# Decay matrices of a chunked delta rule: masked by an added matmul, or clipped on ScalarE and selected on GpSimd

## The chip, the core and the metric

The kernel runs on one core of one Trainium2 chip. The metric is device microseconds of one launch. The times of before come from three runs; the profile comes from one more execution, taken by the hardware profiler.

## The reference, cut to what matters

The program is two transformer-like blocks on a sequence of 512 tokens with width 1024. The first block mixes by a gated delta rule in 8 heads, forward and backward, with a context of 256 tokens whose final states start the 512 tokens; beside it runs a pooling mixer. The second block is two layers of feed-forward, attention, convolution and a gate. The change touches only the delta rule's decay matrix:

```python
g = jnp.cumsum(g.reshape(bsz, nh, n, CHUNK), axis=-1)
incl = jnp.tril(jnp.ones((CHUNK, CHUNK), bool))
decay = jnp.exp(jnp.where(incl, g[..., :, None] - g[..., None, :], -jnp.inf))
a_mat = jnp.where(strict, jnp.einsum('bhncd,bhnsd->bhncs', kb, k) * decay, 0.0)
...
qk = jnp.einsum('bhncd,bhnsd->bhncs', q, k) * decay
```

Within a chunk, the decay from one token to another is the exponential of a difference of running sums, and zero where the second token isn't before or at the first. The kernel takes chunks of 128 tokens in the place of 64, which gives the same outputs: 2 chunks of context and 4 of the sequence, 6 in all per head and direction.

## The kernel before, in words

Everything lies with channels on the 128 partitions and tokens on the free axis. Every large product is made of three matmuls on operands split into a rounded part and a rest (`mm3`, lines 153 to 158: the rounded weights with both parts of the input, then the rest of the weights). `Stream` (lines 83 to 129) brings the weights in 512 KB pieces (`wraw`, three buffers) and splits each half on ScalarE (`whi`, line 108) and VectorE (`wlo`, line 109), with raised priority.

The first block (`block1`, line 799) prepares constants (lines 842 to 902), norms and modulation, and the gates of all heads at once (lines 1031 to 1079): `G` holds the running sums of g, with tokens on partitions, one column for each of 6 chunks and 16 pairs of direction and head; `GT` holds the same with tokens on the free axis, as two rounded parts.

Then it goes through 8 heads. The steps of a head are `k_in` (project k, convolve it, transpose it, norms), `pre` (decay matrices and the triangular inverse), `v_in`, `q_in` and `weights` (the products of q and k times the decay); in between stand `zproj`, `merge`, `chains` and `finish` of the head before, in the order of `STEPS = 'kzmpvcqwf'` (line 703). `merge` builds the inverse of a 128x128 triangular matrix from its 16x16 blocks in three levels, on TensorE (lines 1263, 1268, 1274) with ScalarE and VectorE between; `chains` runs the 6 chunks forward and backward.

`pre` (line 1179) makes, for each direction d, the tile `e` (E, 128 x 6 x 128). A matmul (line 1192) with a selecting column as weights spreads one row of `GT` over all partitions in PSUM (`Ep`, the pool `mis` of two buffers, 2 chunks and then 4); a second matmul (line 1194) adds the mask, 0 or -2^100, with the identity as weights and the mask repeated along the chunks as the moving operand. Line 1197 then takes Exp of each chunk on ScalarE, with the negated running sum of the row as bias. After both directions, B is E[1] times beta (ScalarE, line 1200), plus E[0] times beta (VectorE, line 1202), times the products of k with itself (`KK`, lines 1206 and 1207). B's 16x16 diagonal blocks go to DRAM and back in another layout (lines 1208 to 1217), VectorE inverts them in 15 steps (lines 1219 to 1221), and DMAs bring the results through DRAM into the diagonals of `Pm` and `Qm` (lines 1226 to 1236), which GpSimd has filled with zeros (line 1232). `merge` of this head works on them, one head later. `E` is also read by `weights` (line 1244).

The tiles E, B, P and Q have two buffers each per tag, and the convolved k (`kT`) of even and odd heads lies in two buffers in turn, so the copy of k for head N+2 (in `conv5`, line 1091) waits for the chains of head N.

The order on each engine's queue is fixed when the program is built: instructions whose operands are expected to be ready are taken by their place in the source, so that matmuls of projections stand between those of merge and chains. All DMAs of these steps are issued from SyncE's queue, in which the loads of the weights also stand.

Of the kernel before, what the change touches and what calls it, by code (L numbers as in the profile page):

```python
# [8 lines left out]
F32R = mybir.dt.float32r  # L9
AF = mybir.ActivationFunctionType  # L10
ALU = mybir.AluOpType
PSUM = bass.MemoryType.PSUM

P = 128
# [18 lines left out]
NEG = -float(2 ** 100)  # L33
# [765 lines left out]
def block1(tc, kk, W, h, xp, hp, xt, ctxt, par1, po, rcnt, prep2):  # L799


    nc = tc.nc
    with ExitStack() as ctx:
        cp = ctx.enter_context(tc.tile_pool(name="b1c", bufs=1))
# [13 lines left out]
        def tmp(name="t", shape=(P, S), dt=F32):  # L818
            return tp.tile(list(shape), dt, tag="t", name=name, bufs=5)
# [22 lines left out]
        def triangle(dst, op, fill, pattern, base=0, cm=1, init=0.0):  # L842
            nc.gpsimd.memset(dst, init)
            nc.gpsimd.affine_select(out=dst, in_=dst, compare_op=op, fill=fill, base=base,
                                    pattern=pattern, channel_multiplier=cm)

        cons = {}
        for d in range(2):
            t = tmp("tri", (P, P))

            triangle(t, ALU.is_ge, 0.0, [[1, P] if d == 0 else [-1, P]], cm=-1 if d == 0 else 1, init=1.0)
            cons["tri", d] = t
            m = tmp("m", (P, P))
            triangle(m, ALU.is_ge, NEG, [[1, P] if d == 0 else [-1, P]], cm=-1 if d == 0 else 1)
            mr = cp.tile([P, P], F32R, name=f"maskr{d}")
            nc.vector.tensor_copy(mr, m)
            cons["maskr", d] = mr
        for b in (16, 32, 64):

            g = 64 // b  # L860
# [3 lines left out]
            for t in range(2):  # L864
                lo = b if t == 0 else 0
                nc.gpsimd.affine_select(out=mv[:, :, t], in_=mv[:, :, t], compare_op=ALU.is_ge, fill=0.0, base=-lo,
                                        pattern=[[-2 * b, g], [0, b]], channel_multiplier=1)
                nc.gpsimd.affine_select(out=mv[:, :, t], in_=mv[:, :, t], compare_op=ALU.is_ge, fill=0.0, base=lo + b - 1,
                                        pattern=[[2 * b, g], [0, b]], channel_multiplier=-1)
# [7 lines left out]
        for base in (0, -64):  # L877
            nc.gpsimd.affine_select(out=zt, in_=zt, compare_op=ALU.not_equal, fill=1.0, base=base,
                                    pattern=[[-1, 16]], channel_multiplier=1)
        nc.vector.tensor_copy(zs, zt)  # L880
        DD = []
        for i in range(1):
# [5 lines left out]
                                    pattern=[[1, 16], [-1, 16]], channel_multiplier=0)  # L888
# [4 lines left out]
        cm = sp.tile([P, 2 * KD + 30], F32, name="cm")  # L893
# [146 lines left out]
        def gcol(name):  # L1040
            return sp.tile([P, 6, 16], F32, name=name)
# [13 lines left out]
        for d in range(2):  # L1055
            nc.tensor.matmul(pg[:, d * 48:d * 48 + 48], lhsT=cons["tri", d], rhs=g_[:, :, 8 * d:8 * d + 8], start=True, stop=True)
        nc.tensor.matmul(pg[:, 96:192], lhsT=onesm, rhs=g_, start=True, stop=True)
        G, negG, eG, negeG, etail, egl = (gcol(n) for n in ("G", "negG", "eG", "negeG", "etail", "egl"))
        for d in range(2):
            nc.vector.tensor_copy(G[:, :, 8 * d:8 * d + 8], pg[:, d * 48:d * 48 + 48].rearrange("p (c r) -> p c r", r=8))  # L1060
        gl = pg[:, 96:192].rearrange("p (c r) -> p c r", r=16)
        nc.vector.tensor_scalar(negG, G, -1.0, None, op0=ALU.mult)
        nc.scalar.activation(eG, G, AF.Exp)
        nc.vector.tensor_scalar(negeG, eG, -1.0, None, op0=ALU.mult)
        nc.vector.tensor_tensor(etail, gl, G, op=ALU.subtract)
# [113 lines left out]
        def pre(st):  # L1179


            hd = st.hd
            kc = [st.kT[:, tok(c)] for c in range(6)]
            st.E = E = []
            for d in range(2):
                r = 8 * d + hd
                e = cp.tile([P, 6, P], F32, tag="E", name="E", bufs=2)
                E.append(e)
                for a, b in ((0, 2), (2, 6)):
                    n = (b - a) * P  # L1190
                    ps = pmis("Ep")
                    nc.tensor.matmul(ps[:, :n], lhsT=zs[:, r:r + 1].to_broadcast([80, P]), rhs=GT[:, a * P:b * P],
                                     start=True, stop=False)
                    nc.tensor.matmul(ps[:, :n].rearrange("p (c r) -> p c r", r=P), lhsT=kk.identr,
                                     rhs=cons["maskr", d].unsqueeze(1).to_broadcast([P, b - a, P]), start=False, stop=True)
                    for c in range(a, b):
                        nc.scalar.activation(e[:, c], ps[:, (c - a) * P:(c - a) * P + P], AF.Exp, bias=negG[:, c, r:r + 1])
            st.B = cp.tile([P, 6, P], F32, tag="B", name="B", bufs=2)
            for c in range(6):
                scaled("B", st.B[:, c], E[1][:, c], st.ga[:, 0, c, 1:2])  # L1200
            for c in range(6):
                nc.vector.scalar_tensor_tensor(st.B[:, c], E[0][:, c], st.ga[:, 0, c, 0:1], st.B[:, c], op0=ALU.mult, op1=ALU.add)
            for a, b in ((0, 2), (2, 6)):
                ps = pmis("KK")
                for c in range(a, b):
                    nc.tensor.matmul(ps[:, (c - a) * P:(c - a) * P + P], lhsT=kc[c], rhs=kc[c], start=True, stop=True)
                nc.vector.tensor_tensor(st.B[:, a:b], st.B[:, a:b], ps[:, :(b - a) * P].rearrange("p (c r) -> p c r", r=P), op=ALU.mult)
            db = dp.tile([6, 8, 16, 16], F32, tag="db", name="db")
            for b in range(8):
                s = slice(16 * b, 16 * b + 16)  # L1210
                nc.sync.dma_start(db[:, b].rearrange("m r c -> r m c"), st.B[s, :, s])

            lt, X = DD[0]
            lr = tmp("lr")[0:48, :256].rearrange("p (r c) -> p r c", c=16)
            nc.sync.dma_start(lr, db.rearrange("m b r c -> (m b) r c"))
            nc.sync.dma_start(lt[64:112], db.rearrange("m b r c -> (m b) r c"))
            nc.vector.tensor_copy(lt[0:48], lr.rearrange("p r c -> p c r"))
            T = tmp("T")[0:112, :256].rearrange("p (r c) -> p r c", c=16)
            for i in range(1, 16):
                nc.vector.tensor_tensor(T[:, :i, :i], lt[:, i, :i].unsqueeze(2).to_broadcast([112, i, i]), X[:, :i, :i], op=ALU.mult)  # L1220
                nc.vector.tensor_reduce(X[:, i, :i], T[:, :i, :i].rearrange("p j c -> p c j"), axis=AX, op=ALU.add, negate=True)

            XT = tmp("XT")[0:112, :256].rearrange("p (r c) -> p r c", c=16)
            nc.vector.tensor_copy(XT, X.rearrange("p r c -> p c r"))

            st.P = cp.tile([P, 6, 2, P], F32, tag="P", name="Pm", bufs=2)
            st.Q = cp.tile([P, 6, 2, P], F32, tag="Q", name="Qm", bufs=2)
            for dst, f, w in ((st.P, (1, XT), (0, X)), (st.Q, (0, X), (1, XT))):
                dq = dp.tile([6, 2, 8, 16, 16], F32, tag="dq", name="dq")
                for p0, (t, y) in ((0, f), (64, w)):  # L1230
                    nc.sync.dma_start(dq[:, t].rearrange("m b r c -> m b (r c)"), y[p0:p0 + 48].rearrange("p r c -> p (r c)"))
                nc.gpsimd.memset(dst, 0.0)
                fl = dst.rearrange("p c t r -> p (c t) r")
                for b in range(8):
                    s = slice(16 * b, 16 * b + 16)
                    nc.sync.dma_start(fl[s, :, s], dq[:, :, b].rearrange("m t r c -> r (m t) c"))
# [342 lines left out]
```

## Time and profile before

| | |
|---|---|
| median of 3 runs | 2981.84 us (2981.61 to 2983.72) |
| the profiled execution, its time | 2982.64 us |
| its span, first to last instruction | 2980.9 us |
| TensorE busy | 2935.6 us, 98% |
| VectorE busy | 1914.2 us, 64% |
| ScalarE busy | 1302.4 us, 44% |
| GpSimd busy | 48.1 us, 2% |
| DMA | 268.77 MB, 90 GB/s in the mean |
| granted clock of TensorE, mean | 0.995 of 2.4 GHz |

The span goes from the first to the last instruction of the program; the time of the execution lies a little above it. PE is TensorE's matmuls, PEld its loads of weights (beside them), DVE VectorE, ACT ScalarE, POOL GpSimd, SP SyncE; a q behind the name is the engine's sequencer. The ends of matmuls are modelled, and one matmul's printed duration overlaps the next one's: what a matmul costs in a row of them is the distance between two starts. The heads of the first block lie between some 70 and 600 us; the second block follows from there to the end.

### The profile page before, as it was taken

Reading aid. Unit: us, or ns where it says so; the run is one execution under the profiler, and the core shown is the slowest. Engines: PE = TensorE matmul, PEld = TensorE weight load, DVE = VectorE, ACT = ScalarE, POOL = GpSimd, SP = SyncE. Lnnn points to the kernel's source line nnn. Section 1 sums busy time; section 2 is a strip of 40 time slices with the busy share of each in tenths; the row PEclk is TensorE's granted clock in tenths of the full one; section 3 lists DMA queues with packets and bytes.
Section 4 is the critical chain, followed back from the end, with each engine's and each line's share of the span. In section 5 each row is a group of like instructions: output and inputs, shape, how many; then the busy total and the mean of one; then the engine's idle time right before and its main releaser. Section 6 shows DMA issues by size and latency. Waiting matters only on the chain.

```text
span 2980.9 us, 37957 instructions
## 1 busy us (share of the span) xinstructions
PE 2935.6 (98%) x13980; PEld 2393.3 (80%) x13980; DVE 1914.2 (64%) x3778; ACT 1302.4 (44%) x2395; POOL 48.1 (2%) x105
## 2 busy tenths in 40 slices
PE   7999999999999999999999999999999999999998
PEld 4888888778888887688888888888888688888886
DVE  6788888777544469886543447544469886543446
ACT  5667766435323335544432335323335544432333
POOL 1000000000000000000000000000000000000000
PEclk9999999999999999999999999999999999999999
DMA  5211123332333332123333333333332123233232
GB/s 202 67 46 46 45 57 106 93 92 90 94 99 95 97 99 85 50 85 99 93 99 99 95 96 101 98 99 97 95 99 84 50 87 99 92 99 99 93 99 85
DMA packets 112970, 268.77 MB, mean 90 GB/s; under 512 B 43536, under 2 KB 47120, under 8 KB 112784
## 3 DMA queue, kind: packets, MB, share of 16 engines
q1 hardware_dynamic: 111760, 266.28, 28.9%
q8 instruction: 110, 1.80, 0.3%
q14 instruction: 76, 0.62, 0.1%
q0 software_dynamic: 1024, 0.07, 0.0%
HBM read 262.17 MB, written 4.06 MB: 89 GB/s over the span
## 4 chain that ended last, share of the span: by engine, by line
PE 95%; DVE 2%; ACT 2%; issue 1%; DMA 0%; DVEq 0%; SPq 0%; ACTq 0%
PE pj L158 17%; PE pj L156 17%; PE pj L157 17%; PE fo L156 5%; PE fo L158 5%; PE fo L157 5%; PE px L156 3%; PE px L157 3%; PE px L158 3%; PE o L485 1%; PE wo L157 1%; PE mP L1268 1%; PE mX L1263 1%; PE wo L158 1%; PE wo L156 1%; PE chn L1315 1%
## 5 line engine op out<-in xcount | busy, mean ns | idle before, releaser
L108 ACT CAST whi<-wraw 128x512 fp32r<-128x512 f32 x914 | 567.0, 621 | 1158.5 <-PE pj L157 700.3
L109 DVE TENSOR_TENSOR wlo<-wraw,whi 128x512 fp32r<-128x512 f32 x914 | 627.4, 687 | 449.4 <-ACT whi L108 427.0
L157 PE MATMUL pj<-xl,whi 128*128 128x512 f32 x1712 | 673.3, 393 | 0.0
L156 PE MATMUL pj<-xh,whi 128*128 128x512 f32 x1712 | 671.1, 392 | 0.9 <-DVE h L1504 0.9
L158 PE MATMUL pj<-xh,wlo 128*128 128x512 f32 x1712 | 670.2, 391 | 0.0
L158 PEld LDWEIGHTS pj<-xh,wlo 128*128 128x128 f32 x1712 | 322.2, 188 | 67.8 <-issue 2.3
L157 PEld LDWEIGHTS pj<-xl,whi 128*128 128x128 f32 x1712 | 322.3, 188 | 66.8 <-issue 2.7
L156 PEld LDWEIGHTS pj<-xh,whi 128*128 128x128 f32 x1712 | 322.4, 188 | 65.9 <-ACT whi L108 1.3
L157 PE MATMUL fo<-gl,whi 128*128 128x512 f32 x704 | 274.1, 389 | 0.0
L158 PE MATMUL fo<-gh,wlo 128*128 128x512 f32 x704 | 274.1, 389 | 0.0
L156 PE MATMUL fo<-gh,whi 128*128 128x512 f32 x704 | 274.1, 389 | 0.0
L419 DVE SCALAR_TENSOR_TENSOR cy<-ca,par,cy 128x489 f32<-128x489 f32 (+17 forms) x240 | 169.5, 729 | 1.5
L157 PE MATMUL px<-xl,whi 128*128 128x512 f32 x392 | 160.3, 409 | 0.0
L158 PE MATMUL px<-xh,wlo 128*128 128x512 f32 x392 | 160.0, 408 | 0.0
L156 PE MATMUL px<-xh,whi 128*128 128x512 f32 x392 | 159.2, 406 | 0.0
L158 PEld LDWEIGHTS fo<-gh,wlo 128*128 128x128 f32 x704 | 132.2, 188 | 27.4
L157 PEld LDWEIGHTS fo<-gl,whi 128*128 128x128 f32 x704 | 132.2, 188 | 27.4
L156 PEld LDWEIGHTS fo<-gh,whi 128*128 128x128 f32 x704 | 132.2, 188 | 27.3
L340 DVE TENSOR_TENSOR fb<-pj,R 128x512 f32<-128x512 f32 x88 | 60.8, 691 | 129.3 <-PE pj L158 129.3
L337 DVE TENSOR_TENSOR fa<-pj,R 128x512 f32<-128x512 f32 x88 | 60.8, 691 | 125.2 <-PE pj L158 123.2
L156 PE MATMUL pj<-nh,whi 128*128 128x512 f32 x352 | 137.5, 391 | 0.0
L157 PE MATMUL pj<-nl,whi 128*128 128x512 f32 x352 | 137.2, 390 | 0.0
(431 smaller groups left out, 4486.3 us busy)
## 6 DMA issues: line engine op xcount, KB each, us to landing
wraw<-in_w_dram SPq DMA_DIRECT2D x465, 512.0 KB
mw<-in_w_dram SPq DMA_DIRECT2D x16, 512.0 KB
raw<-in_xt_dram SPq DMA_DIRECT2D x8, 256.0 KB
h<-in_xt_dram SPq DMA_DIRECT2D x8, 256.0 KB
out_dram<-fin SPq DMA_DIRECT2D x8, 256.0 KB
rawc<-in_ctxt_dram SPq DMA_DIRECT2D x2, 512.0 KB
db<-B SPq DMA_DIRECT2D x64, 6.0 KB
Pm<-dq SPq DMA_DIRECT2D x64, 12.0 KB
```

The source lines that it names most:

```text
L108: nc.scalar.copy(hi, src)
L109: nc.vector.tensor_tensor(lo, src, hi.bitcast(F32), op=ALU.subtract)
L156: nc.tensor.matmul(ps, lhsT=wh, rhs=xh, start=start, stop=False)
L157: nc.tensor.matmul(ps, lhsT=wh, rhs=xl, start=False, stop=False)
L158: nc.tensor.matmul(ps, lhsT=wl, rhs=xh, start=False, stop=stop)
L337: nc.vector.tensor_tensor(a, pa, R, op=ALU.mult)
L340: nc.vector.tensor_tensor(b, pb, R, op=ALU.mult)
L419: nc.vector.scalar_tensor_tensor(yy[:, s:], ca[cb][:, :S - s], pcol("conv_w", l, cb, j), yy[:, s:], op0=ALU.mult, op1=ALU.add)
L485: nc.tensor.matmul(po_[r, kb * P:], lhsT=vt[kb][:, hp * P + 64 * i:hp * P + 64 * i + 64], rhs=pts[i], start=kb == 0, stop=kb == 3)
L1263: nc.tensor.matmul(pX[:, o], lhsT=st.B[:, m0 + m], rhs=alt(st.Q, m0 + m), start=True, stop=True)
L1268: nc.tensor.matmul(pP[:, o], lhsT=Xt[:, m], rhs=alt(st.P, m0 + m), start=True, stop=True)
L1315: nc.tensor.matmul(pa, lhsT=st.kN[:, c], rhs=y2, start=True, stop=True)
```

## The change

The mask's matmul is gone, and with it the two masks. Each chunk's read of PSUM on ScalarE now computes Relu(G - Ep), the difference with its sign turned and clipped at zero, with `G` itself as bias, so that `negG` is gone too. Then one Exp with scale -1 runs in place over all 6 chunks of a direction (768 columns), and one `affine_select` on GpSimd, also in place over all 6 chunks, writes zeros on the side of the diagonal where the mask stood (by d, above or below).

```diff
-            m = tmp("m", (P, P))
-            triangle(m, ALU.is_ge, NEG, [[1, P] if d == 0 else [-1, P]], cm=-1 if d == 0 else 1)
-            mr = cp.tile([P, P], F32R, name=f"maskr{d}")
-            nc.vector.tensor_copy(mr, m)
-            cons["maskr", d] = mr
...
-        nc.vector.tensor_scalar(negG, G, -1.0, None, op0=ALU.mult)
...
                     nc.tensor.matmul(ps[:, :n], lhsT=zs[:, r:r + 1].to_broadcast([80, P]), rhs=GT[:, a * P:b * P],
-                                     start=True, stop=False)
-                    nc.tensor.matmul(ps[:, :n].rearrange("p (c r) -> p c r", r=P), lhsT=kk.identr,
-                                     rhs=cons["maskr", d].unsqueeze(1).to_broadcast([P, b - a, P]), start=False, stop=True)
+                                     start=True, stop=True)
                     for c in range(a, b):
-                        nc.scalar.activation(e[:, c], ps[:, (c - a) * P:(c - a) * P + P], AF.Exp, bias=negG[:, c, r:r + 1])
+
+                        nc.scalar.activation(e[:, c], ps[:, (c - a) * P:(c - a) * P + P], AF.Relu, scale=-1.0, bias=G[:, c, r:r + 1])
+                nc.scalar.activation(e, e, AF.Exp, scale=-1.0)
+
+                nc.gpsimd.affine_select(out=e, in_=e, compare_op=ALU.is_ge, fill=0.0, base=0,
+                                        pattern=[[0, 6], [1 - 2 * d, P]], channel_multiplier=2 * d - 1)
```

## Rows read from the trace of the kernel before

**Rows 1.** The page, first part: busy time, share and instructions of each engine.

```profile
PE 2935.6 (98%) x13980; PEld 2393.3 (80%) x13980; DVE 1914.2 (64%) x3778; ACT 1302.4 (44%) x2395; POOL 48.1 (2%) x105
```

**Rows 2.** The page: the chain that ended last, shares of the span.

```profile
PE 95%; DVE 2%; ACT 2%; issue 1%; DMA 0%; DVEq 0%; SPq 0%; ACTq 0%
```

**Rows 3.** Table of stretches: length, then busy us of each engine, granted clock, DMA.

```profile
core 0: us, PE busy (x) PEld busy (x) DVE busy (x) ACT busy (x) POOL busy (x), PEclk, DMA share, GB/s
118.00:510.00 392.00, 388.71 (x2547) 334.52 (x2546) 335.69 (x1092) 264.00 (x630) 18.91 (x15) 1.00 0.22 58
510.00:600.00 90.00, 88.71 (x478) 69.64 (x478) 65.13 (x161) 41.58 (x91) 0.00 (x0) 1.00 0.31 91
```

**Rows 4.** TensorE's waits from 70 to 530 us, longest: total, times, longest.

```profile
PE mP L1268 <- DVE Xt L1264: 1.0, 1, 1.0
```

**Rows 5.** Line 1194 (ns min/median/max), then the timeline of TensorE in head 2.

```profile
L1194 PE MATMUL Ep<-maskr,identr x32: 281/338/404, 76.1 to 468.4; 128*128 128x256 f32 x16, 128*128 128x512 f32 x16
...
185.91 0.40 PE L1194 MATMUL Ep<-maskr,identr 128*128 128x512 f32 x1
186.15 0.28 PE L158 MATMUL pc<-cx,wlo 128*128 128x256 f32 x1
...
188.60 0.28 PE L1194 MATMUL Ep<-maskr,identr 128*128 128x256 f32 x1
188.72 0.39 PE L158 MATMUL px<-xh,wlo 128*128 128x512 f32 x1
```

**Rows 6.** Timeline of ScalarE, head 3: start, us, idle before in brackets.

```profile
239.25 1.28 ACT L1197 ACT_TABLE_LOAD   x1
...
242.22 1.28 ACT L1139 ACT_TABLE_LOAD   x1
...
244.22 1.28 ACT L1197 ACT_TABLE_LOAD   x1
245.51 1.66 ACT L1197 ACTIVATE E<-Ep,negG 128x128 f32<-128x128 f32 x6
247.02 0.43 ACT L830 ACTIVATE B<-E,ga 128x128 f32<-128x128 f32 x1
```

**Rows 7.** ScalarE's groups by shape, 70 to 530 us: busy us, mean ns.

```profile
L1197 ACT ACT_TABLE_LOAD x16 | 20.5, 1283 | 0.3
...
L828 ACT COPY u<-px 128x512 f32<-128x512 f32 x23 | 13.2, 581 | 0.7 <-PE px L158 0.7
...
L828 ACT COPY u<-pc 128x256 f32<-128x256 f32 x15 | 5.6, 374 | 5.8 <-PE pc L158 3.3 <-PE chn L1302 2.5
```

**Rows 8.** GpSimd's groups by shape, whole span: busy us, mean ns.

```profile
L1232 POOL MEMSET Pm<- 128x1536 f32 x8 | 11.1, 1382 | 159.9 <-PE chn L1311 121.3 <-PE pc L158 25.5 <-DVE cx L169 13.2
...
L844 POOL TENSOR_SCALAR_AFFINE_SELECT tri<-tri 128x128 f32<-128x128 f32 x2 | 0.6, 293 | 0.0
...
L887 POOL TENSOR_SCALAR_AFFINE_SELECT Xx<-Xx 112x256 f32<-112x256 f32 x1 | 0.5, 514 | 0.0
```

**Rows 9.** Timeline of GpSimd, from 200 to 230 us.

```profile
202.82 1.38 POOL L1232 MEMSET Qm<- 128x1536 f32 x1 [26.23 <-PE mX L1263]
228.47 1.39 POOL L1232 MEMSET Pm<- 128x1536 f32 x1 [24.27 <-PE chn L1311]
```

**Rows 10.** Timelines of SyncE and TensorE, heads 2 and 7: Qm's issues, merge's first matmuls.

```profile
226.13 5.29 SPq L1236 DMA_DIRECT2D Qm<-dq  x8
...
234.64 0.83 PE L1263 MATMUL mX<-Qm,B 128*128 128x128 f32 x6
...
511.77 4.73 SPq L1236 DMA_DIRECT2D Qm<-dq  x8
...
521.41 0.83 PE L1263 MATMUL mX<-Qm,B 128*128 128x128 f32 x6
```

**Rows 11.** Timelines of SyncE and VectorE, head 0: the read-back's issue, and its reader.

```profile
94.11 0.32 SPq L1215 DMA_DIRECT2D lr<-db  x1
...
96.75 0.38 DVE L1217 COPY Lt<-lr 48x256 f32<-48x256 f32 x1 [1.69 <-DMA lr<-db]
```

**Rows 12.** ScalarE's waits from 70 to 530 us: total, times, longest.

```profile
ACT u L828 <- PE chn L1302: 2.5, 4, 0.6
```

More of the change, by code (lines that the diff above doesn't have):

```diff
@@ L1057, in block1 @@
         nc.tensor.matmul(pg[:, 96:192], lhsT=onesm, rhs=g_, start=True, stop=True)
-        G, negG, eG, negeG, etail, egl = (gcol(n) for n in ("G", "negG", "eG", "negeG", "etail", "egl"))
+        G, eG, negeG, etail, egl = (gcol(n) for n in ("G", "eG", "negeG", "etail", "egl"))
         for d in range(2):
```

## The prediction

> **What bounds the kernel now.** I read the page first: TensorE is busy 2935.6 of 2980.9 us [rows 1], and the chain of work that ended last lies on it for 95% [rows 2]. Then the table of stretches, for the stage that the change touches: from 118 to 510 us, where heads 1 to 7 run their decay matrices, TensorE is busy 388.71 of 392 us, so only 3.3 us of idle time can be won there without taking work away, while ScalarE has 264 and VectorE 336 us [rows 3]. TensorE's own list of waits there has a longest entry of 1.0 us [rows 4]. The granted clock is 1.00 in both stretches, its upper level of 2.4 GHz. So time falls if TensorE has less to do, as long as the longer way round on the other engines doesn't make it wait.
>
> **What is removed.** The mask matmul stands in the trace 32 times, 16 of 256 and 16 of 512 columns [rows 5]. Its printed duration (338 ns) overlaps the next matmul's, so the price is the distance from its start to the next start: 186.15 - 185.91 = 0.24 us for 512 columns, 188.72 - 188.60 = 0.12 us for 256 [rows 5]. 16 x (0.24 + 0.12) = 5.76 us off TensorE, 0.72 us a head, all in stretches where it has no idle time to speak of. This is the one gain that I count. The two masks' preparation and the negation of G (a few instructions on GpSimd and VectorE, once, before 70 us) lie beside matmuls and loads, and I count nothing for them; if that cover were gone they would add some tenths of a us.
>
> **What is added on ScalarE.** The twelve reads of PSUM per head stay, with Relu in the place of Exp. I take the same duration: a set of six took 1.66 us with Exp [rows 6]. New are two Exp over 768 columns per head. No row shows 768 columns with constant operands; a copy of 256 columns took 374 and one of 512 took 581 ns [rows 7], 0.81 ns a column, so 0.581 + 256 x 0.00081 = 0.79 us each. That is 1.6 us a head, 13 us in all, in the densest part of ScalarE's work: in head 3, from the first table load at 239.25 us to the scaling of B at 247.02 us, no row shows idle time before it [rows 6]. It also delays what is queued behind on ScalarE, the weight casts and merge's copies, by up to 0.8 us at a time; TensorE has several matmuls of one unit of weights as cover.
>
> **What is added on GpSimd.** Two selects over 128x768 per head. A 128x128 select took 293 ns, the 112x256 one with a pattern of two levels 514 ns [rows 8]. That is 1.73 ns an element, so 0.514 + 512 x 0.00173 = 1.40 us; I take this one, as the new pattern has two levels too. The lower bound is from the filling of 128x1536, which only writes: half of 1382 ns, 0.69 us [rows 8]. GpSimd is nearly free (18.9 us in 392 [rows 3]). Its queue holds the fillings of Qm and Pm, which wait for buffers of earlier heads: they run at 202.82 and 228.47 us [rows 9], before head 3 needs its first select (after 242 us [rows 6]), so a select should find the queue empty.
>
> **How much later B is ready.** The first half's Exp is 0.79 us ahead of the second half's reads on the same queue; the second half's Exp takes 0.79; its select 1.40, and only then may ScalarE scale B. Sum 3.0 us, the hops between engines (tenths of a us) in it. Bounds: 4.3, if Relu needs a table load of its own (1.283 us [rows 7]); 1.0, if a select takes 0.69 (2 x 0.79 + 0.69 = 2.3) and one table load falls away (2.3 - 1.3). VectorE's step of B waits for that scaling, and behind it on VectorE's queue stand the weight splits and merge's additions; both product tiles of KK stay in PSUM until B is there, and the two buffers of that pool are what the value transposes wait for next.
>
> **Who is late then.** B goes by DMA to DRAM and back, through the substitution, and by DMA into Pm and Qm, which merge multiplies. All of that moves by the same 3.0 us. I measure the slack at its end, from the last issue of Qm to merge's first matmul: 231.42 to 234.64 us in head 2, 516.50 to 521.41 in head 7, and 3.5, 4.1, 5.6 and 5.4 us in heads 3 to 6 between them, six heads [rows 10]. Landing takes 2.3 us of it: the read-back issued by 94.43 us ends VectorE's wait at 96.75 [rows 11]. So the slack is 0.9, 1.2, 1.8, 3.3, 3.1 and 2.6 us, and a delay of 3.0 overshoots it by 2.1, 1.8, 1.2, 0, 0 and 0.4: 5.5 us. TensorE isn't idle in that gap today; it runs projections, and can run more of them early, but what it runs there it doesn't have later, between the steps of merge. With neither end shown by a row, I count half, 2.75 us, and keep 0 and 5.5 as the ends.
>
> **Sum.** Against the profiled execution (2982.64 us, 1.7 around the span): 2982.64 - 5.76 + 2.75 = 2979.6. That execution lies 0.80 above the median of the three runs (2981.84), so 2978.8 to be measured. With the ends of the idle time the forecast's own range is 2976.1 to 2981.6, almost all of it within 0.2% (5.96 us, about what a measurement can tell from no change).
>
> **A rule against the change.** The rows show no GpSimd instruction that reads SBUF beside a busy VectorE, since the selects of before run once, ahead of the work. The Trainium skill says in "GPSIMD Engine Reference", Specifications, that GpSimd shares its SBUF interfaces with VectorE, with contention for VectorE instructions that have two SBUF inputs. By it VectorE would lose at most the selects' own 2.8 us a head, out of the 8 us a head that it has free in this stage ((392 - 336) / 7 [rows 3]); the sum would stay, and the slower rival below would gain weight.
>
> **Rivals.**
> *Faster: ScalarE gets shorter in spite of the Exp.* Today each half has its own load ahead of its first read, with the Sqrt's load between them: 239.25, 242.22, 244.22 [rows 6], 16 loads for E in 8 heads [rows 7]. After the change only the long Exp needs that table, and it comes later; if both halves' Exp fall behind the Sqrt, a head needs one load less, 1.28 us, which pays for most of the 1.6. B is then only some 1.7 us late, most of the slack holds, and the 3.3 us of idle time may go too: 2981.84 - 5.76 = 2976.1 down to 2972.8, say 2974.5. Against it: the order of the queues follows the source and readiness, and Sqrt was ready between the halves in head 3. The Trainium skill, "ScalarE: Activation LUTs", Table sets, says that relu lies in every set; by that the reads need no load, as this rival and my forecast have it, and no row of before shows a Relu.
> *No gain: the change doesn't do what it says for the time.* The 5.5 us become idle time in full: 2981.84 - 5.76 + 5.5 = 2981.6. This is the upper end of the forecast and shares its chance.
> *Slower: the loop through kT's buffers sets the pace.* The copy of k for head N+2 waits for the last matmul of head N's chains: ScalarE waited for them four times, though 0.6 us at most [rows 12]. From there the way goes through E, B, substitution, Pm and merge to the chains of N+2, two heads on. If nothing in this lap gives, each lap is 3.0 us longer, and heads 1, 3, 5 and 7 make three laps: 9.0 us. TensorE's saving is then not collected, since it waits for the chain anyway: 2981.84 + 9.0 = 2990.8. It decides from the point where TensorE runs out of projections to put in the gap before merge. For it: the slack is below 3.0 us in four of six heads. Against it: TensorE is 99% busy in the stage, so the lap is today stretched by queueing on TensorE, and that part can shrink.
>
> **How the numbers follow.** Forecast 0.58, faster rival 0.20, slower rival 0.22. The prediction is the forecast's 2978.8. The range runs from 2973 (most of the faster rival, down to its full gain) to 2990 (the slower one without its last us). Faster by over 0.2% takes in the faster rival only, 0.20; within 0.2% the forecast, 0.58; slower by over 0.2% the slower rival, 0.22.
>
> **What would show it.** Right: 32 matmuls fewer; TensorE's starts around the Ep matmuls closer by 0.24 and 0.12 us; Exp rows near 0.8 us and selects near 1.4 us, 16 each; TensorE's idle time in the stage up by about 3 us; Qm's last issue up to 3 us later against the chains' end. Wrong: selects beyond 2 us or waiting behind a filling of Pm or Qm; merge's first matmul waiting for a DMA; 8 loads for E instead of 16 (the faster rival); waits of TensorE for vNp or mX above 1 us in each head (the slower). A change of order far from these lines, which the build may choose anew everywhere in the first 600 us, would make the sum wrong in a way that no row of before shows.

## The result and the profile after

The changed kernel takes 3014.11 us (median of 4 runs, 3013.87 to 3015.99) against 2982.63 of the kernel before: the ratio is 1.0105, 95% interval 1.0093 to 1.0118. It is slower by 31.5 us, where 2978.8 was forecast and 2990 was the upper end.

The page of the kernel after, busy time and the chain that ended last (line numbers are each kernel's own from here on):

```profile
PE 2944.8 (98%) x13948; PEld 2395.2 (80%) x13948; DVE 1914.6 (64%) x3775; ACT 1320.7 (44%) x2415; POOL 62.2 (2%) x117
...
PE 90%; ACT 4%; DVE 3%; issue 1%; DMA 1%; SPq 0%; POOL 0%; DVEq 0%; ACTq 0%; POOLq 0%
```

There are 32 matmuls fewer [rows 1], and yet TensorE is busy for 9 us more; the chain leaves TensorE for 10% of its length, where it had left it for 5% [rows 2]. The table of stretches of the kernel after, columns as in [rows 3], then the longest entries of TensorE's waits from 70 to 660 us (total, times, longest):

```profile
118.00:510.00 392.00, 369.99 (x2342) 314.19 (x2341) 311.21 (x1003) 266.20 (x607) 29.87 (x26) 0.97 0.21 55
...
PE mQ L1271 <- ACT new L828: 9.7, 9, 1.8
PE mP L1265 <- DVE Xt L1261: 6.9, 8, 1.1
```

From 118 to 510 us TensorE is idle for 22.0 us, where it had been for 3.3 [rows 3], and the granted clock is 0.97 in the mean, where it had been 1.00. Up to 530 us the wait that led the list before was a single one of 1.0 us [rows 4]; now merge waits 17 times, for its copy on ScalarE and its product on VectorE. The clock goes down in stretches of the kind shown next (kernel after):

```profile
440.00:455.70 15.70, 12.77 (x81) 11.76 (x80) 11.14 (x41) 8.98 (x19) 1.75 (x2) 0.78 0.20 60
455.70:462.60 6.90, 6.66 (x47) 5.72 (x46) 5.06 (x13) 4.41 (x14) 0.50 (x1) 1.00 0.61 186
```

In 15.7 us TensorE is idle for 2.9 us, and a mean of 0.78 means some 6.9 us of it at the lower level, 1.2 GHz. There, matmuls of 256 columns start 0.21 us apart (at 449.57, 449.78 and 450.00 us), and 0.12 us apart from 452.07 us on, at the upper level. The stretches at 1.2 GHz make 27 us between 70 and 660 us, where before there were none; at half speed that is at most 13.6 us of work lost. The whole of that window, kernel before and kernel after:

```profile
70.00:660.00 590.00, 584.13 (x3540) 492.32 (x3540) 484.28 (x1411) 357.12 (x818) 18.91 (x15) 1.00 0.24 68
```

```profile
70.00:660.00 590.00, 563.71 (x3385) 471.11 (x3383) 462.35 (x1376) 365.25 (x822) 33.82 (x31) 0.98 0.23 64
```

TensorE's idle time went up by 20.4 us. Both together, at most 34 us (some idle time lies within the slow stretches), are about the loss (31.5), with little or nothing of the masks' saving to be seen.

The parts themselves came out near the forecast. Groups of E, kernel after (ns min/median/max):

```profile
L1190 ACT ACTIVATE E<-Ep,G x96: 349/372/410, 77.1 to 502.4; 128x128 f32<-128x128 f32 x96
L1191 ACT ACTIVATE E<-E x16: 842/845/893, 82.9 to 505.0; 128x768 f32<-128x768 f32 x16
L1193 POOL TENSOR_SCALAR_AFFINE_SELECT E<-E x16: 862/864/1697, 83.8 to 505.9; 128x768 f32<-128x768 f32 x16
```

So the question is why 1.7 us a head more on ScalarE and two selects a head of 0.86 us cost 31.5 us in all.

### The profile page after: what moved, and what is told of

Its sections match the earlier page's. It is cut to its first block, busy times and chain, and to the rows that moved or that the text cites. A ratio compares the mean times of both kernels' runs of the same rounds, so it can differ in the third digit from the quotient of the medians.

```text
span 3012.5 us, 37907 instructions
## 1 busy us (share of the span) xinstructions
PE 2944.8 (98%) x13948; PEld 2395.2 (80%) x13948; DVE 1914.6 (64%) x3775; ACT 1320.7 (44%) x2415; POOL 62.2 (2%) x117
## 4 chain that ended last, share of the span: by engine, by line
PE 90%; ACT 4%; DVE 3%; issue 1%; DMA 1%; SPq 0%; POOL 0%; DVEq 0%; ACTq 0%; POOLq 0%
PE pj L156 17%; PE pj L157 17%; PE pj L158 17%; PE fo L158 5%; PE fo L156 5%; PE fo L157 5%; PE px L156 2%; PE px L157 2%; PE px L158 2%; PE o L485 1%; PE wo L157 1%; PE wo L158 1%; PE wo L156 1%; PE mP L1265 1%; PE pt L477 1%
```

## Experiments

Each comparison is with the kernel before, run on the same chip. A recorded expectation stands ahead of each result, in a quotation. Four theories were in play first: the long Exp and its table loads hold ScalarE's queue (S); the select does it (G); the order that the build chose anew does it (O); and, after the first four runs, the loop through kT's two buffers (L). From e12 on there is Q: in a queue whose order is fixed, TensorE pays for whatever is put on ScalarE ahead of a result that it needs. e18 adds B: each head pays what B is late.

### The parts alone, in orders that the build chose

**e1_no_mask**: the kernel before without its 32 mask matmuls.

```diff
-                                     start=True, stop=False)
-                    nc.tensor.matmul(..., lhsT=kk.identr, rhs=cons["maskr", d]..., start=False, stop=True)
+                                     start=True, stop=True)
...
-    nc.scalar.activation(e[:, c], ..., AF.Exp, bias=negG[:, c, r:r + 1])
+    nc.scalar.activation(e[:, c], ..., AF.Exp, scale=0.0, bias=G[:, c, r:r + 1])
```

> The kernel before without the mask's matmuls and nothing in their place: Exp reads PSUM with scale 0 and bias G, so that the decays are not those of the reference (one value per row, no zeros beside the diagonal). Theory S (ScalarE: the 16 long Exp and the table loads around them stand ahead of merge's copies, TensorE waits for these and then gets half the clock): only the 5.76 us of TensorE's time go, 2975 to 2979 us. Theory G (GpSimd: the select makes B late, and merge with it): the same. Theory O (any new order of the queues costs, whatever the change): 2990 us or more, as after.

**e2_long_exp** (the mask kept, Relu and the long Exp, no select), **e3_select** (the kernel before and the two selects, nothing else) and **e4_no_select** (the change without its selects):

```diff
+                        nc.scalar.activation(e[:, c], ..., AF.Relu, scale=-1.0, bias=G[:, c, r:r + 1])
+                nc.scalar.activation(e, e, AF.Exp, scale=-1.0)
...
+                nc.gpsimd.affine_select(out=e, in_=e, compare_op=ALU.is_ge, fill=0.0, ...)
```

> The kernel before with ScalarE's part of the change alone: mask matmul kept, Relu out of PSUM and one Exp over 768 columns, no select on GpSimd. Theory S: nearly all of the loss, and no saving on TensorE: 3005 to 3022 us, with TensorE waiting for merge's copies (mQ) over 5 us in all and stretches at half the clock between 130 and 600 us. Theory G: within 6 us of before. Theory O: 2990 us or more.

> The kernel before with GpSimd's part of the change alone: mask matmul and Exp per chunk kept, the select added behind them (it writes zeros where zeros are). Theory S: 2980 to 2989 us, since 0.86 us of select and its hops lie within the slack. Theory G: over 3000 us. Theory O: 2990 us or more.

> The changed kernel without its select; the zeros beside the diagonal are left out (ones stand there). Theory S: within 8 us of the changed kernel, 3004 to 3016 us, with the waits for merge's copies still there. Theory G: the saving appears, 2975 to 2982 us. Theory O: 2990 us or more.

| run | time, us | ratio, 95% interval |
|---|---|---|
| e1_no_mask | 2987.48 | 1.0014 (1.0005 to 1.0023) |
| e2_long_exp | 3010.11 | 1.0089 (1.0074 to 1.0104) |
| e3_select | 3016.18 | 1.0109 (1.0092 to 1.0126) |
| e4_no_select | 3016.31 | 1.0109 (1.0094 to 1.0124) |

The saving alone makes the kernel 4 us slower, outside the bounds of all three theories, and either half of the added work alone costs about as much as the whole change (e2 27 us, e3 and e4 33). S and G both fail as sole causes: e4 without selects and e3 without long Exps lose the same. Nothing adds up here. Each edit also gets an order of its own, so these runs can't tell work from order.

### The loop, and other orders

**e5_after_three_kT** gives kT a third buffer, **e8_no_mask_three_kT** does so in e1; **e6_batched** puts both long Exps behind all twelve Relus in the source; **e7_priority** raises the priority of the whole stretch.

```diff
-        for i in range(4):
+        for i in range(5):
...
-                u = us[blk % 2]
+                u = us[(0, 1, 4)[blk % 8 % 3]]
```

> The changed kernel with a third buffer for kT (the copy of k for head N+2 no longer waits for the last chains matmul of head N; the room comes from the 128-column ones matrix, which becomes a temporary). The computation is whole. Theory L (the loop through kT's two buffers is paid three times, 9 us each): TensorE's idle time between 70 and 660 us falls from 27 us to under 10, no stretch of that stage stays at the half clock, and the time falls to 2980 to 2992 us. Rival S (what costs is the merge's copies that stand behind the long Exp and the table loads in ScalarE's queue, and the loop only follows): the waits mP <- Xt and mQ <- new stay at some 1 us twice per merge, and the time stays at 3003 us or above.

> The kernel before without its 32 mask matmuls, six Exps per direction that read the decay of their own column alone (the decays themselves are left out of this run), and with the third kT buffer. Theory L: with the loop open, the 5.76 us of TensorE work that the mask matmuls took are collected: 2974 to 2980 us, against 2987 for the same edit with two buffers. Rival O: 2983 us or above.

> The changed kernel, computation whole, with one edit of order: the twelve Relus of both directions first, then the two long Exps and the two selects, so that one table load can stand for both Exps. Theory L: the stretch from kNp to the last Exp gets shorter by up to 3 us per loop (one to two table loads of 1.28 us and what stands between them), three loops, and the half clock goes partly: 2995 to 3006 us. Rival S: same direction, but the gain shows in the merge's waits for Xt and new, with the loop's length unchanged. If neither the loop nor the merge gets shorter, the time stays within 4 us of 3014.

> The changed kernel, computation whole, with the whole stretch from the difference matmuls to the product with KK put ahead of other work in the build's order. Theory L: the loop loses what it waits for in the queues of ScalarE and VectorE (select to B*KK 8.5 us, 4.8 before the change): 2 to 5 us per loop, so 2996 to 3008 us. Rival O (any new order of this stage costs about 1%, the length of the loop does not matter): 3010 to 3018 us, with the loop shorter or not.

Measured: e5 3016.37 us (ratio 1.0110, 1.0095 to 1.0125), e8 3000.01 (1.0054, 1.0039 to 1.0069), e6 3017.45 (1.0114), e7 3041.01 (1.0190). ScalarE's waits in the kernel after hold this row, the copy of k that waits for the chains two heads back (before: 2.5 us in four times [rows 12]):

```profile
ACT u L828 <- PE chn L1299: 5.1, 7, 1.6
```

In e5 that row is gone, and the time stays; L's bounds are missed in all four runs. These too have orders of their own, but two readings from e9 below, in the old order, settle it: there ScalarE waits 2.4 us for the chains, in four times, as before, and heads 0 and 1, which no earlier head's chains hold up, already lose 3.8 and 3.4 us between their transposes of k and of the value. So theory L, the prediction's slower rival, falls. And e8 does nearly the same work as e1, in another order and with a third buffer, for 12.5 us more, a first hint of what an order can cost.

### The old order, held

To part work from order, the next kernels hold every engine's queue in a given order, by edges that set the order of issue and nothing else; ORDER is the order in which the build had put the kernel before (in e10 the changed kernel).

```diff
+def pin(tc, nc):
+    place = ...
+    last = {}
+    for n in place:
+        i = ins[n]
+        e = str(i.engine)
+        if e in last:
+            tc.add_manual_dep(i, last[e].name, ...)
+        last[e] = i
...
         tile_main(tc, *args, off1, off2)
+        pin(tc, nc)
```

> The changed kernel, computation whole, with each engine's queue held in the order that the build chose for the kernel before: 12972 matmuls, 3727 VectorE, 2202 ScalarE and all DMA instructions stand in the old order; each long Exp follows its direction's last Relu and each select its Exp; 8 scalings and additions of B that had stood ahead of a select go right behind it. Theory O (the loss is the new order that the build chose, 1019 of 12972 matmuls moved against the others, not the work of the change): TensorE's idle time from 70 to 660 us is under 12 us, there is no half clock, and the time is 2974 to 2985 us. Theory L (a loop that must be longer by the long Exps and selects whatever the order): 3000 us or above, with the idle time above 20 us.

> The kernel before, computation whole, its work unchanged (mask matmuls, Exp with bias, no long Exp, no select), with each engine's queue held in the order that the build chose for the changed kernel; each mask matmul follows its Ep matmul. Theory O: the order alone costs what the change cost, so 3003 to 3018 us, with TensorE idle for over 15 us from 70 to 660 us. Theory L: without the long Exps and selects the loop is short again in any order: 2990 us or below.

> The kernel before without its 32 mask matmuls, and with Exps that read the decay of their own column alone (the decays themselves are left out of this run), every queue held in the order of the kernel before. Both theories: nothing is longer and nothing moved, so the 5.76 us of the mask matmuls are collected: 2975 to 2979 us, against 2987 for the same edit in an order of its own. If it is above 2981, the saving itself was misjudged: the mask matmuls stood where TensorE would wait anyway.

> The kernel before with Relu reads and the long Exp (mask matmuls kept, no select; computation whole), every queue held in the order of the kernel before, each long Exp behind its direction's last read. Theory Q (in a fixed order, what is put into ScalarE's queue between the reads of Ep and the next silu or copy of merge is paid by TensorE one for one): two Exps of 0.85 us in 8 heads are 13.5 us, and with half-clock stretches after the waits 2995 to 3010 us; TensorE's list of waits then names ScalarE (KK <- E, mQ <- new, vNp <- u) for most of its idle time. Theory L (only the length of the way from k to merge counts): each of three loops is 1.7 us longer, 2986 to 2990 us.

> The kernel before with the selects alone (mask matmuls and direct Exp kept; computation whole), every queue held in the order of the kernel before, each select behind its direction's last Exp. Theory Q: ScalarE has no more work, but its scaling of B stands in its queue and waits for the second select, 0.86 us and two hops in 8 heads, so some 8 us: 2987 to 2997 us, again with ScalarE in TensorE's list of waits. Theory L: three loops of 0.9 us each, 2983 to 2987 us. Rival G (selects on GpSimd disturb VectorE through shared SBUF access): VectorE's busy time goes up by more than 5 us against the kernel before and the waits name VectorE.

| order | work | time, us | against before | ratio, 95% interval |
|---|---|---|---|---|
| old | e11, masks' matmuls gone | 2983.13 | -0.3 | 1.0001 (0.9992 to 1.0010) |
| old | e13, selects added | 2995.04 | +11.7 | 1.0038 (1.0023 to 1.0053) |
| old | e12, long Exps added | 3005.61 | +22.3 | 1.0073 (1.0058 to 1.0088) |
| old | e9, the whole change | 3012.53 | +29.1 | 1.0100 (1.0083 to 1.0117) |
| the changed kernel's | e10, the old work | 3023.23 | +39.8 | 1.0134 (1.0119 to 1.0149) |

With the order held, the parts add up to within 5 us: 11.7 + 22.3 - 0.3 = 33.7 against 29.1. The work costs its 29 us in the old order too, where theory O had asked for 2974 to 2985 us, so a loss of this size needs no new order. But the new order is bad by itself: the old work loses 39.8 us in it (e10), more than the changed work's 31.5. The two prices don't add, and how the changed kernel's own 31.5 us part into work and order is not shown. The edges themselves cost nothing that shows: the trace of e11 has, on TensorE, the 13948 matmuls that before has without the masks, in the same order, and as many instructions on VectorE, ScalarE and GpSimd. e12 and e13 lie within the bounds of Q and outside those of L. And e11 settles the saving: by its interval it lies between a gain of 2.4 us and a loss of 3.0, not at 5.76.

**Where the mask matmuls' time went (e11).** TensorE's timeline in head 2, first the kernel before (the mask matmul itself, at 185.91, stands in [rows 5]), then e11:

```profile
185.59 0.48 PE L1192 MATMUL Ep<-GT,zsel 80*128 80x512 f32 x1
...
187.19 0.40 PE L157 MATMUL px<-xl,whi 128*128 128x512 f32 x1
187.43 0.54 PE L1274 MATMUL mQ<-ident,new 128*128 128x128 f32 x3
```

```profile
185.63 0.48 PE L1192 MATMUL Ep<-GT,zsel 80*128 80x512 f32 x1
185.95 0.28 PE L158 MATMUL pc<-cx,wlo 128*128 128x256 f32 x1
...
187.00 0.39 PE L157 MATMUL px<-xl,whi 128*128 128x512 f32 x1
187.51 0.55 PE L1272 MATMUL mQ<-ident,new 128*128 128x128 f32 x3
```

The projection behind the mask starts 0.20 us earlier (185.95 for 186.15), by nearly the price read from [rows 5]. At 187.00 it is still 0.19 ahead. Then mQ, which multiplies a copy from ScalarE, starts at 187.51 for 187.43: all is given back within 1.6 us. It is the copy that holds it: on ScalarE the copy runs for 0.47 us from 186.90 in before and from 186.99 in e11, and mQ starts 0.06 and 0.05 us after its end. Compared matmul by matmul over all heads, e11 is 0.75 us late at 71 us and 0.95 us early at the end of the last chains: 1.7 of the 5.76 us stay, and the rest is given back in small steps at mQ, mP, KK and Ep.

**Where the added work goes (e9, e12, e13).** TensorE's waits, 60 to 660 us, in e9 and then e12:

```profile
PE KK L1203 <- ACT E L1190: 9.2, 6, 2.2
PE mQ L1271 <- ACT new L828: 7.8, 6, 1.9
PE vNp L1155 <- ACT u L1105: 6.4, 3, 2.6
```

```profile
PE KK L1207 <- ACT E L1197: 7.2, 6, 1.9
PE mQ L1275 <- ACT new L828: 4.6, 6, 1.0
PE vNp L1161 <- ACT u L1111: 3.9, 3, 1.9
```

All three are waits for ScalarE: for the reads that free a PSUM buffer for KK, for merge's copy, for the silu of the value. ScalarE in head 3 of e9 shows what stands ahead of them (compare [rows 6]):

```profile
255.25 0.84 ACT L1191 ACTIVATE E<-E 128x768 f32<-128x768 f32 x1
256.11 1.28 ACT L1133 ACT_TABLE_LOAD   x1
257.40 0.21 ACT L1133 ACTIVATE ssk<-ssk 128x6 f32<-128x6 f32 x1
257.52 0.46 ACT L828 COPY new<-mP 128x384 f32<-128x384 f32 x1
257.88 1.67 ACT L1190 ACTIVATE E<-Ep,G 128x128 f32<-128x128 f32 x6
259.56 1.28 ACT L1191 ACT_TABLE_LOAD   x1
260.85 0.84 ACT L1191 ACTIVATE E<-E 128x768 f32<-128x768 f32 x1
262.66 0.40 ACT L830 ACTIVATE B<-E,ga 128x128 f32<-128x128 f32 x1 [0.96 <-POOL E L1193]
262.97 0.60 ACT L108 CAST whi<-wraw 128x512 fp32r<-128x512 f32 x1
263.48 0.69 ACT L830 ACTIVATE B<-E,ga 128x128 f32<-128x128 f32 x2
264.07 0.46 ACT L828 COPY new<-mP 128x384 f32<-128x384 f32 x1
```

and TensorE's waits of 0.5 us and more in the same stretch:

```profile
258.03 0.55 PE L1271 MATMUL mQ<-ident,new 128*128 128x128 f32 x3 [1.08 <-ACT new L828]
264.58 0.55 PE L1271 MATMUL mQ<-ident,new 128*128 128x128 f32 x3 [1.80 <-ACT new L828]
```

The copy at 257.52 stands behind the first long Exp (0.84), and TensorE waits 1.08 us for it. The copy at 264.07 stands behind the second one and behind the scaling that waits 0.96 us for the select, 1.80 together, and TensorE waits 1.80. Here the queue passes its delay on whole. In e13 ScalarE's own list has the same wait, with no work added to ScalarE at all:

```profile
ACT B L830 <- POOL E L1198: 9.3, 8, 1.8
```

Eight waits of 9.3 us in all, against 11.7 us of time lost. VectorE is busy 1918.0 us in e13 for 1914.2, below the 5 us more that its rival G asked for.

### Attempts to take the delay away

**e14_clip_on_VectorE** gives the 96 reads to VectorE, with both long Exps behind all of a head's reads, in an order of the build's own; **e15_scale_on_GpSimd**, **e16_batched_in_before_order** and **e17_both_in_before_order** start from e9; **e18_sqrt_behind_B** moves the small Sqrt, with its table loads, from between the Exps to behind the scaling of B. The edits of e14, e15 and e18, one after the other:

```diff
-    nc.scalar.activation(e[:, c], ..., AF.Relu, scale=-1.0, bias=G[:, c, r:r + 1])
+    nc.vector.tensor_scalar(e[:, c], ..., G[:, c, r:r + 1], 0.0, op0=ALU.subtract, op1=ALU.min)
...
-    scaled("B", st.B[:, c], E[1][:, c], st.ga[:, 0, c, 1:2])
+    nc.gpsimd.tensor_scalar(st.B[:, c], E[1][:, c], st.ga[:, 0, c, 1:2], None, op0=ALU.mult)
...
+    nc.vector.reciprocal(ss[:, 4], ss[:, 0])
-    rec = ss[:, 2].unsqueeze(2).to_broadcast([P, 6, 2])
+    rec = ss[:, 4].unsqueeze(2).to_broadcast([P, 6, 2])
```

> The changed kernel, computation whole, with the 96 clipping reads of Ep on VectorE (difference and minimum with zero in one instruction) in the place of ScalarE's Relu, and both long Exps and selects behind them; the order is the build's own. Theory Q: ScalarE loses 12 x 0.37 = 4.5 us a head and TensorE's waits for ScalarE (mQ <- new, KK <- E, vNp <- u) fall below 5 us in the stage: 2978 to 2995 us. Rival D (VectorE, 86% busy in the stage before, becomes the queue that TensorE waits for): 3000 us or above, with mP <- Xt at the head of the list. Theory O (any order other than the old one costs about 1%): 3005 us or above with waits on both engines.

> The changed kernel in the old order as in e9, computation whole, with the six scalings of B per head on GpSimd in the place of ScalarE (6 x 0.39 = 2.3 us a head less on ScalarE, against 1.7 more by the long Exps; and the scaling no longer holds ScalarE's queue while it waits for the select). Theory Q: the waits mQ <- new and vNp <- u fall from 14 us to under 5; KK <- E (9 us) stays, since the first direction's Exp still stands between the reads: 2990 to 3000 us. Rival L (the way from k to merge alone counts): that way gets no shorter, so 3007 us or above.

> The changed kernel in the old order as in e9, computation whole, with both long Exps behind the last of the twelve reads of a head (the second direction's first, then its select, then the other's). Theory Q: KK <- E goes (9.2 us to under 2) because its PSUM buffer is freed before the long Exps; mQ <- new and vNp <- u stay or grow, since both Exps and the scaling that waits for the select stand ahead of them: 2998 to 3010 us. Rival L: the way to B is no shorter than in e9, so no gain beyond 3 us: 3009 us or above.

> e15 and e16 together: scaling of B on GpSimd, both long Exps behind all reads, the old order, computation whole. Theory Q: all three waits go, idle time from 70 to 660 us below 12 us and no half clock: 2982 to 2990 us, about the kernel before. Rival L: B is ready some 3 us later than before in every head, so three loops of 3 us at least: 2992 us or above.

> The changed kernel in the old order as in e9, computation whole, with one thing more: the Sqrt of k's norms (6 columns), which stands between the two directions' Exps on ScalarE and takes a table load of 1.28 us there and another one for the Exp after it, stands behind the last scaling of B (beta over the norm is made from the squares before it, so that B doesn't wait for it). The way from kNp to B then loses 1.28 + 1.28 + 0.21 = 2.8 us a head, about the 3.0 us that the change adds. Theory B (each head pays, about one for one, what B is late, whichever work makes it late): the way is 16.1 us a head against 15.9 before and 18.9 in e9, no half clock, waits KK <- E and vNp <- u below 5 us together: 2979 to 2990 us. Rival (the long Exp and the select cost by themselves, by their load on ScalarE's queue and on SBUF): ScalarE has only one load less, 8 x 1.28 = 10 us, so 2998 us or above.

Measured: e14 3007.14 us (ratio 1.0078, 1.0062 to 1.0095), e15 3017.59 (1.0114), e16 3008.00 (1.0080), e17 3018.93 (1.0120), e18 3018.99 (1.0121). In all but e16 the time that the theory then held had asked for was missed (e14 came out as its rival D had it, and within the time of O, which its own order can't rule out; e15 and e17 lie within the bounds of L, e18 within those of its rival), and the lists of waits say why. The longest row of e14, and the two longest of e15, e16 and e18:

```profile
PE mP L1264 <- DVE Xt L1260: 7.6, 10, 1.7
```

```profile
PE vNp L1155 <- DVE B L1204: 9.3, 3, 3.9
PE KK L1203 <- ACT E L1190: 9.1, 6, 2.2
```

```profile
PE vNp L1155 <- ACT u L1105: 8.7, 3, 3.7
PE mQ L1271 <- ACT new L828: 7.0, 4, 3.4
```

```profile
PE vNp L1155 <- ACT u L1105: 10.3, 4, 3.5
PE KK L1203 <- ACT E L1190: 9.1, 6, 2.2
```

Where an edit removes the wait that it was aimed at, a neighbour takes its place. In e15 ScalarE's waits for the select are gone and mQ's wait falls from 7.8 to 2.4 us, but the scaling takes 0.60 us on GpSimd for 0.40, VectorE's additions stand and wait for it, and TensorE waits for VectorE. In e16 the wait of KK is off the list (9.2 us in e9), since its buffer is free before the long Exps, and the silu waits longer behind them. In e17 the wait of KK is gone too, and TensorE waits 13.2 us for B on VectorE. In e18 the wait of KK, which was to shrink, stays at 9.1, and the silu now waits for the Sqrt that was put ahead of it.

One number goes with the time lost in all runs in the old order, to within 3 us; it says where the time goes, not why. The stretch of a head from its first kNp matmul (transposes of k) to the end of its last vNp matmul (transposes of the value), read from TensorE's rows, is 18.85 us before, mean of 8 heads; head 3 of before and of e9, first and last start:

```profile
L1128 PE MATMUL kNp<-ident,u x6: 273/273/273, 236.4 to 237.8; 128*128 128x128 f32 x6
...
L1161 PE MATMUL vNp<-ident,u x6: 271/272/273, 253.2 to 254.8; 128*128 128x128 f32 x6
```

```profile
L1122 PE MATMUL kNp<-ident,u x6: 272/272/273, 249.4 to 250.9; 128*128 128x128 f32 x6
...
L1155 PE MATMUL vNp<-ident,u x6: 270/272/273, 268.6 to 270.2; 128*128 128x128 f32 x6
```

| run, old order | growth of kNp to vNp, us a head | times 8 | growth of all 8 heads (first kNp to last chains), us |
|---|---|---|---|
| e11 | -0.23 | -1.8 | -1.7 |
| e13 | +1.38 | 11.0 | 11.0 |
| e12 | +2.65 | 21.2 | 21.1 |
| e16 | +3.32 | 26.6 | 25.8 |
| e9 | +3.38 | 27.1 | 27.0 |
| e17 | +4.07 | 32.5 | 34.2 |
| e18 | +4.12 | 32.9 | 32.4 |
| e15 | +4.29 | 34.3 | 34.5 |

In eight kernels the change of the stage lies in this stretch, once per head, to within 1.7 us, and no other stretch gives it back. What is *late* in it differs: in e18 B is ready 0.7 us a head earlier than in e9 (18.2 us after the first kNp, not the 16.1 that the edit was meant to reach) and the time is longer. So theory B, that B's lateness is the whole cause, falls as well; delays on ScalarE (e9) and on VectorE (e15) between kNp and vNp both count.

## Why the prediction was wrong, point by point

- *TensorE bounds the stage, so time falls if it has less to do.* Wrong in this stretch. It was read from 388.71 of 392 us busy [rows 3]. In e11 it had 5.76 us less to do by the price from [rows 5], and the kernel was 0.3 us faster, within the interval. This is the first term that failed: 5.76 us counted, nothing measured. Where it was followed (head 2 of e11), a matmul taken out left a shorter row of projections ahead of the same result of ScalarE.
- *Relu, the long Exp, the select.* Relu costs what Exp did and needs no table load: none of the 96 rows has one. The Trainium skill, "ScalarE: Activation LUTs", Table sets, says that relu is in every set; this trace agrees. The long Exp took 0.845 us (0.79 estimated), the select 0.86 (1.40 taken, 0.69 as the lower bound).
- *B is ready 3.0 us later.* Right in the old order, in part by luck: from kNp to the end of the product with KK it is 18.86 us in e9 for 15.86, a mean of heads that differ by 1.9 to 5.3 us, while two Exps and a select as measured make only 2.55. In the changed kernel's own order it is 7.5 us later (23.32), as the build put other work ahead.
- *Half of a 5.5 us overshoot is paid.* This is the second term that failed, and the one that made the loss. It looked for the delay at its far end, in merge's first matmul, and set it against the slack there. The delay was paid long before, between kNp and vNp: 27 us in e9 against 2.75. The sentence that hid it is in the part on ScalarE: the copies queued behind are late "by up to 0.8 us at a time; TensorE has several matmuls of one unit of weights as cover". No row had been shown for that cover. The trace would have given it: between the table loads of [rows 6] stands a copy of merge, and the mQ that multiplies it follows on TensorE (timelines of ScalarE, then TensorE, head 3 of before):

```profile
243.72 0.48 ACT L828 COPY new<-mP 128x384 f32<-128x384 f32 x1
```

```profile
244.34 0.49 PE L1274 MATMUL mQ<-ident,new 128*128 128x128 f32 x3
```

  The copy ends at 244.20: the cover was 0.14 us, not several matmuls. It is so in the other heads: of the 32 copies of merge of this kind in the kernel before, 28 end less than 0.3 us ahead of their mQ, the median 0.08 us.
- *What TensorE runs early, it doesn't have later.* Named, and counted as half. In the runs in the old order nothing is run early: TensorE waits where it stands (1.80 us in head 3 of e9), and what is lost between kNp and vNp isn't caught up in the rest of the head (the table above).
- *The clock.* Not in the sum. In e12, e9 and the changed kernel 10, 14 and 27 us of the stage ran at 1.2 GHz, at most 5, 7 and 14 us of the loss. There TensorE is idle for 21, 29 and 26 us from 70 to 660 us; e13, with 15 us, kept 2.4 GHz.
- *The rule on GpSimd's shared SBUF access.* In the rows it is small: in e15 VectorE's addition of B, beside GpSimd's scaling, took 0.450 us for 0.346 (rows in the last section), and of the 16 selects of the changed kernel three took 1.01, 1.09 and 1.70 us for 0.86, each begun beside a convolution on VectorE. That is the contention that the Trainium skill names in "GPSIMD Engine Reference", Specifications. In e9 two selects were longer, by 1.1 us together, against 29.1 us lost.
- *The faster rival* asked for 8 loads of E's table fewer. There are 15 for 16, and silu's loads went from 15 to 20 from 70 to 660 us: 53 loads for 49. In the old order (e9) it is 12 for 16 with silu's 15 as before, four loads fewer in all, and the time still rose by 29 us.
- *The slower rival* had the right sign and the wrong mechanism. It gave 9.0 us for three loops through kT's buffers; e5 opened that loop, and nothing changed. Each of eight heads pays (2 to 6 us each in e9), not each of three loops, and by what the queues delay, not by what B is late.
- *What would make it wrong:* waits above 1 us in each head, for vNp or mX, were named for the slower rival. The changed kernel has none; its waits are for mQ and mP, up to 1.8 and 1.1 us, and in e9 vNp waits above 1 us in three heads of eight. The change of order, named last, was there as well. It isn't needed for the loss (29.1 us in the old order, 31.5 in the new), but it costs by itself (e10).

What stays open: whether any order exists in which the changed work costs nothing. Every order tried (the build's own, also from another order of the source, and the old one with four rearrangements) cost some 24 us or more. No version tried beats the kernel before. Open is also the size: in e12 16 long Exps (13.5 us) and at most 5.1 us of the slower clock make 18.6 of 22.3 us, in e13 the waits for the selects 9.3 of 11.7, and the rest was not traced.

## What to carry to other kernels

A TensorE that is 99% busy in a queue of fixed order is not a TensorE with work to spare: before pricing an edit, walk the queue of the engine that gets the new work, name each result behind it that TensorE waits for, and ask how many matmuls stand ahead of that wait as cover. If the wait has no cover, charge the delay once per iteration and in full (here the runs lost somewhat more than that), and add the half-clock stretches that such waits can bring; if a removed matmul stood right ahead of such a wait, count little or nothing of its saving. To part the price of work from the price of a new order, hold the old order and add the parts one at a time.

## What the runs showed of the hardware

Groups of B (ns min/median/max): VectorE's addition in the kernel before, then GpSimd's scaling and the same addition in e15.

```profile
L1202 DVE SCALAR_TENSOR_TENSOR B<-E,ga,B x48: 339/346/352, 85.1 to 478.7; 128x128 f32<-128x128 f32 x48
```

```profile
L1197 POOL TENSOR_SCALAR B<-E,ga x48: 592/602/798, 89.9 to 510.3; 128x128 f32<-128x128 f32 x48
L1199 DVE SCALAR_TENSOR_TENSOR B<-E,ga,B x48: 336/450/459, 90.5 to 513.8; 128x128 f32<-128x128 f32 x48
```

A scaling of 128x128 takes 0.60 us on GpSimd, where ScalarE took 0.40 (the first one of head 3 in e9), and it makes VectorE's addition beside it 0.10 us longer. A select over 128x768 takes 0.86 us on GpSimd, less than the two smaller ones of [rows 8] had led to expect (1.40).
